# adaLN shift and scale of tiles 0, 1 and 5 as pairs from TensorE, products and tables on GpSimd, loads in order of need

## The chip, the cores and the metric

The kernel runs on one core of a Trainium2 chip. The metric is the device time of one execution in microseconds, here the median of the runs shown. The engines that matter are TensorE (PE in the profile, its weight loads PEld), VectorE (DVE), ScalarE (ACT), GpSimd (POOL) and SyncE (SP), which issues all DMAs of this kernel.

## The reference

Two layers of a decoder trunk over 256 tokens of width 1024, all in f32. What matters here is how a layer begins: the vector c gives, through `silu` and `w_mod`, a shift and a scale for each of the 1024 features, and the normed x is scaled, shifted and sent through one combined input projection.

```python
c_act = jax.nn.silu(c)
for l in range(DEPTH):
    mod = c_act @ w_mod[l] + b_mod[l]
    sh1, sc1, g1, sh2, sc2, g2 = jnp.split(mod, 6, axis=-1)
    h = modulate(rms_norm(x, mix_norm_g[l]), sh1, sc1)   # h*(1+sc1) + sh1
    y = token_mixer(h, cos_a, sin_a, cos_b, sin_b, w_in[l], ...)
    x = x + g1[:, None, :] * y
    h = modulate(rms_norm(x, ffn_norm_g[l]), sh2, sc2)
    x = x + g2[:, None, :] * channel_mixer(h, w_up[l], ffn_dw_w[l], ffn_dw_b[l], w_down[l])
```

The mixer's branches (MLA, MoBA, a convolution of 31 taps behind a GLU) use rope tables, that is the cosine and sine of positions times frequencies.

## The kernel before

The features lie on partitions: 1024 features are eight tiles of 128 (`k` = 0 to 7), and x is held as 128 x 8 x 256. Products are made in three passes for f32 accuracy: each operand is split into a rounded part and a rest (`hh` and `hl` for h, `whi` and `wlo` for a weight), and TensorE computes hi times hi, lo times hi and hi times lo (L315, L316 and L318 in `flush`).

A weight comes from memory into a buffer `raw` (one load on SP's queue), ACT makes `whi` (L231), DVE subtracts for `wlo` (L232). The function `take` does this a fixed number of weights ahead (`AHEAD0 = 2` in the first stage); `raw`, `whi` and `wlo` have four buffers each.

Layer 0 begins with a stage of its own, to about 60 us. c becomes `cact` (silu) and a row of it on every partition, `crow`. The squares of x are summed, and GpSimd's power makes rstd (`rs`). Of the modulation, the scale of tiles 0 to 3 comes from TensorE: `mod_first` (L441) loads four pieces of 512 KB, multiplies them with `cact` as stationary operand, 32 columns for each of four column groups of the array (L453), copies, transposes (L460) and adds the bias (L463). The shift of these tiles, and both for tiles 4 to 7, come from DVE: `prepare_tile` loads a row tile of 512 KB (`wmr`) for each and takes its dot with `crow` in one SCALAR_TENSOR_TENSOR with an accumulator (L816, a "dot" below), then adds the bias (L818), multiplies x by rstd into `xn` (L827, the tile `mq` in rows) and makes the gain (L823, `gs`).

The loop over the eight tiles then has ACT make h (L891, `e`) and `hh` (L892), DVE `hl` (L893), and TensorE two projections: `latents(k)` (a weight of 672 columns, 12 matmuls into `psb` banks) and `conv_in(k)` (1024 columns, 24 matmuls into four `psa` banks). Behind the loop follow the evacuations of the latents, the GLU (`glu`: tanh on ACT, `upad` on DVE), and QKV's first projection, which needs two `psa` banks.

Each engine works its instructions in the order of the program. The order is made when the kernel is built, by a scheduler that follows the source's order, dependencies and its own estimates; `issue_after(i)` puts the instructions of a block behind `i` on the same engine. So an instruction that waits holds up all that stand behind it on its engine. That goes for SP's queue too: a load that waits for its buffer holds up the loads behind it. Before the first tile PE works through `warm` matmuls (L338, "fillers" below) that nothing reads; tile 0's `latents` stand behind the last of them.

Of the kernel before, what the change touches and what calls it, by code (L numbers as in the profile page):

```python
# [158 lines left out]
def trunk_kernel(ctx, tc, xT, crow, ccol, pos, invf, modb_d, cols_d, grow_d, wmh, wmr, wm, win1, wqkv,  # L159
# [61 lines left out]
    def split(raw, lead):  # L221
# [6 lines left out]
        with ExitStack() as es:  # L228
            for i in (pins.pop(0) if pins else hold[0] or []):
                es.enter_context(tc.issue_after(i))  # L230
            ac.activation(hi, raw, AF.Copy)  # L231
            ve.tensor_tensor(lo, raw, hi.bitcast(F32), op=ALU.subtract)  # L232
# [207 lines left out]
    def mod_first(l, r, after):  # L440

        raws = []
        for i, tag in enumerate(("qkT", "lh0", "qkT", "lh1")):
# [4 lines left out]
        yield
        acc = psa()
        with tc.issue_after(after[0].ins):  # L450
            for k in range(KD):
                for c in range(4):
                    last = te.matmul(acc[32 * c:32 * c + 32, 0:P], cact[:, k:k + 1].to_broadcast([P, 32]),  # L453
                                     raws[k // 2][:, k % 2, c * P:(c + 1) * P], start=(k == 0), stop=(k == KD - 1),
                                     tile_position=(0, 32 * c))
# [3 lines left out]
        pt = psa()  # L459
        tr = te.transpose(pt[:, 0:P], g[:, 0:P], ident)  # L460
        with tc.issue_after(tr.ins):
            wlast[:] = [warm(wbank[0], WARM0[2])]
        yield ve.tensor_tensor(mod[l][:, r * 8:r * 8 + 4], pt[:, 0:P].rearrange("p (c m) -> p c m", c=4)[:, :, 0],  # L463
# [1090 lines left out]
```

## Time and profile before

| | us |
|---|---|
| median of three runs | 902.13 (901.48 to 904.43) |
| the profiled execution | 905.91 |
| its span | 903.7 |

| first stage, profiled execution | us from the span's start |
|---|---|
| four loads of `wmh`, issued | 3.06 to 5.4 |
| first matmul of the modulation | 10.25 |
| fillers | 15.16 to 18.35 |
| first matmul of tile 0 | 18.68 |
| first matmul of tile 7 | 54.84 |
| first matmul of QKV | 60.05 |

A row of a timeline has start, duration, engine, line, operation, the tile that is written and those that are read, shape and count, and in brackets how long the engine had been idle and what ended that. A row with a count over 1 merges instructions that follow each other. Pipelined instructions overlap by some hundredths of a microsecond, so the step from one to the next is a little less than a duration.

### The profile page before, as it was taken

To read this page: it belongs to the slowest core of one execution; us is meant where nothing else is said; L and a number is where in the kernel's file an instruction comes from. 1 tells how busy PE (TensorE), PEld (TensorE's weight loads), DVE (VectorE), ACT (ScalarE), POOL (GpSimd) and SP (SyncE) were. 2 spreads that over 40 slices of the span, in tenths; PEclk is the share of its full clock that TensorE was granted. 3 is DMA by queue.
4 is the path that set the end of the run, shared out by engine and by line. 5 is a ranking of instruction groups with operands and counts; after the bars stand their busy time and mean duration, and the time that the engine had idled before them with its cause. 6 is when DMAs were issued, how large, how long until landed. Compare 5 with 4: busy or idle time off the path is not lost.

```text
span 903.7 us, 18611 instructions
## 1 busy us (share of the span) xinstructions
PE 884.4 (98%) x7247; PEld 839.6 (93%) x7247; DVE 808.1 (89%) x1592; ACT 559.3 (62%) x998; POOL 47.0 (5%) x36
## 2 busy tenths in 40 slices
PE   8999999999999999999999999999999999999998
PEld 6888888999997999999989988989999999999998
DVE  6989999999987999999774999999987899998774
ACT  4677588644755655556543676787465777556551
POOL 1010700000000000000000033000000000000000
PEclk8999999999999999999999999999999999999999
DMA  8956535699888889996652666156866576886631
GB/s 320 375 202 205 187 118 175 207 330 316 309 285 286 288 287 314 316 306 228 204 161 77 200 196 200 49 167 230 274 200 209 160 233 188 301 280 205 191 95 47
DMA packets 57976, 201.59 MB, mean 223 GB/s; under 512 B 6944, under 2 KB 8480, under 8 KB 57888
## 3 DMA queue, kind: packets, MB, share of 16 engines
q1 hardware_dynamic: 57888, 200.41, 66.5%
q8 instruction: 57, 0.93, 0.4%
q14 instruction: 31, 0.25, 0.1%
HBM read 199.33 MB, written 1.05 MB: 222 GB/s over the span
## 4 chain that ended last, share of the span: by engine, by line
PE 78%; DVE 11%; DMA 5%; ACT 3%; issue 2%; SPq 0%; POOL 0%; DVEq 0%; ACTq 0%; POOLq 0%
PE psb L315 16%; PE psb L316 15%; PE psb L318 15%; PE psa L315 8%; PE psa L316 8%; PE psa L318 8%; DVE wlo L232 3%; DVE cacc L1141 2%; ACT whi L231 1%; DVE raw L816 1%; PE psa L423 1%; PE psa L734 1%; PE psa L746 1%; DMA raw<-in_win 1%; DMA raw<-in_wmh 1%
## 5 line engine op out<-in xcount | busy, mean ns | idle before, releaser
L231 ACT ACTIVATE whi<-raw 128x1024 fp32r<-128x1024 f32 (+2 forms) x286 | 296.0, 1042 | 194.4 <-PE psb L316 98.5
L232 DVE TENSOR_TENSOR wlo<-raw,whi 128x1024 fp32r<-128x1024 f32 (+2 forms) x286 | 340.3, 1195 | 50.7 <-ACT whi L231 42.4
L315 PE MATMUL psb<-hh,whi 128*128 128x256 f32 x1056 | 256.0, 282 | 0.5 <-ACT p L713 0.3
L316 PE MATMUL psb<-hl,whi 128*128 128x256 f32 x1056 | 253.7, 280 | 0.0
L315 PEld LDWEIGHTS psb<-hh,whi 128*128 128x128 f32 x1056 | 198.9, 189 | 5.0 <-issue 2.6
L316 PEld LDWEIGHTS psb<-hl,whi 128*128 128x128 f32 x1056 | 199.0, 189 | 0.5 <-DVE wlo L232 0.4
L318 PE MATMUL psb<-hh,wlo 128*128 128x256 f32 x1056 | 145.0, 279 | 0.0
L318 PEld LDWEIGHTS psb<-hh,wlo 128*128 128x128 f32 x1056 | 131.7, 188 | 0.8 <-issue 0.8
L1141 DVE SCALAR_TENSOR_TENSOR cacc<-upad,cw,cacc 128x256 f32<-128x256 f32 x240 | 105.8, 478 | 0.4
L315 PE MATMUL psa<-mhl,whi 128*128 128x256 f32 x400 | 94.2, 278 | 0.0
L316 PE MATMUL psa<-mhl,whi 128*128 128x256 f32 x400 | 94.0, 278 | 0.0
L1423 DVE SCALAR_TENSOR_TENSOR e<-psb,fw,e 128x255 f32<-128x255 f32 (+1 forms) x168 | 80.0, 478 | 6.6 <-ACT e L1421 6.0
L536 POOL TENSOR_TENSOR rs<-rs,mhalf 128x8 f32<-128x8 f32 (+3 forms) x26 | 45.5, 1761 | 678.0 <-DVE rs L535 677.9
L315 PEld LDWEIGHTS psa<-mhl,whi 128*128 128x128 f32 x400 | 75.1, 188 | 0.0
L316 PEld LDWEIGHTS psa<-mhl,whi 128*128 128x128 f32 x400 | 75.0, 188 | 0.0
L406 DVE SCALAR_TENSOR_TENSOR raw<-raw,crow 128x1024 f32<-128x1024 f32 x56 | 68.3, 1220 | 0.9 <-DMA raw<-in_wmr 0.9
L1421 ACT ACTIVATE e<-psb,fb,fw 128x256 f32<-128x256 f32 x84 | 46.5, 554 | 23.6 <-DVE e L1423 20.1
L318 PE MATMUL psa<-mhl,wlo 128*128 128x256 f32 x400 | 54.0, 278 | 0.0
L318 PEld LDWEIGHTS psa<-mhl,wlo 128*128 128x128 f32 x400 | 49.5, 188 | 0.0
L1431 ACT ACTIVATE mhl<-e 128x256 fp32r<-128x256 f32 x44 | 18.4, 417 | 39.7 <-DVE e L1429 38.0
L315 PE MATMUL psb<-whi,hh 128*128 128x416 f32 (+1 forms) x96 | 30.9, 350 | 2.9 <-ACT hh L892 2.9
L315 PE MATMUL psa<-hh,whi 128*128 128x256 f32 x128 | 30.0, 281 | 0.0
(295 smaller groups left out, 1522.2 us busy)
## 6 DMA issues: line engine op xcount, KB each, us to landing
raw<-in_wup SPq DMA_DIRECT2D x88, 512.0 KB, 4.9
raw<-in_wmr SPq DMA_DIRECT2D x68, 512.0 KB, 5.4
raw<-in_wdn SPq DMA_DIRECT2D x44, 512.0 KB, 4.6
raw<-in_wgab SPq DMA_DIRECT2D x32, 512.0 KB, 5.0
raw<-in_wqkv SPq DMA_DIRECT2D x24, 512.0 KB, 4.7
raw<-in_wm SPq DMA_DIRECT2D x24, 512.0 KB, 4.7
raw<-in_win SPq DMA_DIRECT2D x16, 512.0 KB, 4.5
raw<-in_wgc SPq DMA_DIRECT2D x16, 512.0 KB, 4.4
```

Source lines behind the costliest of these rows:

```text
L231: ac.activation(hi, raw, AF.Copy)
L232: ve.tensor_tensor(lo, raw, hi.bitcast(F32), op=ALU.subtract)
L315: te.matmul(o, p1[0], p1[1], start=start, stop=False)
L316: te.matmul(o, p2[0], p2[1], start=False, stop=False)
L318: last = te.matmul(o, p3[0], p3[1], start=False, stop=stop)
L406: ve.scalar_tensor_tensor(raw, raw, scale, row, op0=ALU.mult, op1=ALU.mult, accum_out=acc)
L423: te.matmul(acc[32 * c:32 * c + 32, 0:S], cact[:, k:k + 1].to_broadcast([P, 32]), raw[:, c * S:(c + 1) * S], start=(k == 0), stop=(k == KD ...
L536: gp.tensor_tensor(r, r, mhalf[:, :n], op=ALU.pow)
L1141: ve.scalar_tensor_tensor(aj, upad[:, j, t:t + S], cw[:, j * 31 + t:j * 31 + t + 1], aj, op0=ALU.mult, op1=ALU.add)
L1421: ac.activation(t, src, AF.Identity, scale=fw[:, 2, c:c + 1], bias=fb[:, c:c + 1])
L1423: ve.scalar_tensor_tensor(t[:, d:S], src[:, 0:S - d], fw[:, 2 - d, c:c + 1], t[:, d:S], op0=ALU.mult, op1=ALU.add)
L1431: ac.activation(mh, th, AF.Copy)
```

## The change

`TK = (0, 1, 5)` names three tiles whose shift and scale both come from TensorE. For each, `mod_pair` loads two pieces of 512 KB (the columns of shift and scale for this tile, the rows in two halves), multiplies both halves in one pass over the array's four column groups, and a matmul with `pick` adds the halves and turns them to two columns. One bank holds all three results. The other five tiles get both values as dots. In bytes that is six pieces of `wmh` and ten row tiles where there were four and twelve.

```diff
-        raws = []
-        for i, tag in enumerate(("qkT", "lh0", "qkT", "lh1")):
-            t = wk.tile([P, D], F32, tag=tag, ...)
-            sy.dma_start(t, wmh[:, 2 * i:2 * i + 2, :])
...
+        kt, raws = TK[i], []
+        for h in range(2):
+            tag, bufs = (("lh0", "lh1")[h], 1) if i == 1 else ("qkT", 2)
...
+            sy.dma_start(t, wmh[i, :, 4 * h:4 * h + 4, :])
...
+        acc = mbank[0][:, i * 160:i * 160 + 160]
         with tc.issue_after(after[0].ins):
+            for h in range(2):
+                for k in range(4):
+                    for c in range(2):
+                        o = 32 * (2 * h + c)
+                        last = te.matmul(acc[o:o + 32, 0:P], cact[:, 4 * h + k:4 * h + k + 1].to_broadcast([P, 32]),
+                                         raws[h][:, k, c * P:(c + 1) * P], start=(k == 0), stop=(k == 3),
+                                         tile_position=(0, o))
         g = e1()
         ac.activation(g[:, 0:P], acc[:, 0:P], AF.Copy)
         yield last
-        tr = te.transpose(pt[:, 0:P], g[:, 0:P], ident)
+        tr = te.matmul(acc[:, P:P + 2], g[:, 0:P], pick, start=True, stop=True)
+        if i == 0:
+            with tc.issue_after(tr.ins):
+                wlast[:] = [warm(wbank[0], WARM0[2])]
```

The products of x and rstd for tiles 1 to 7, the bases of the rope tables and layer 0's tables go from DVE to GpSimd, and in the source the tables move from behind the loop to behind tile 2. For tile 0, ACT makes `hh` straight from `xn`, and DVE computes h once more for `hl`.

```diff
-                with tc.issue_after(mods0[-1].ins) if k else ExitStack():
-                    ve.tensor_tensor(xn[k // 4][:, k % 4, :], x[:, k, :], bcs, op=ALU.mult)
+            ve.tensor_tensor(xn[0][:, 0, :], x[:, 0, :], bcs, op=ALU.mult)
+            for k in range(1, KD):
+                gp.tensor_tensor(xn[k // 4][:, k % 4, :], x[:, k, :], bcs, op=ALU.mult)
...
-            ve.tensor_copy(dst[:, 0, :, 0:w], cs)
+            gp.tensor_copy(dst[:, 0, :, 0:w], cs)
...
-                    ve.tensor_tensor(t[:, i, :, qk, :], base[:, i, :, :],
+                    (ve if l else gp).tensor_tensor(t[:, i, :, qk, :], base[:, i, :, :],
```

The weights of the stage are loaded two tiles ahead, with three more tags of buffers lent to them (`kv`, `vb`, `lh2`: four buffers, free in this stage), each tile's modulation before its two weights; `grow`, the factors of the tables, comes after tile 4's. Tile 7 does `conv_in` ahead of `latents`. `pins` puts chosen weight splits behind given instructions.

```diff
+    raw_tags = [("raw", 4), ("kv", 2), ("raw", 4), ("vb", 1), ("raw", 4), ("lh2", 1)]
...
+            def load_tile(k):
+                if k in TK:
+                    pes[k] = mod_pair(TK.index(k), lat_last)
+                    step(pes[k])
+                else:
+                    for r in range(2):
+                        raws0[r, k] = wload_row(0, r, k, (SPARE[len(raws0) % 4], 1))
+                preload()
+                preload()
...
+            if k + 2 < KD:
+                load_tile(k + 2)
+            if k == KD - 1:
+                conv_in(k)
+            elif k + 1 in pes and k:
+                lat_last[:] = [convl]
+                step(pes[k + 1])
             with tc.issue_after(wlast[0].ins) if k == 0 else ExitStack():
-                latents(k)
+                lat_last[:] = [latents(k)]
+            if k + 1 in pes and not k:
+                step(pes[k + 1])
...
             if k + 1 < KD:
-                prepare_tile(k + 1)
-            conv_in(k)
+                with tc.issue_after(los[-2].ins if k == 1 else last.ins):
+                    prepare_tile(k + 1)
+                make_tile(k + 1)
+                if k in (0, KD - 2):
+                    pins[:] = [[i.ins for i in tiles[k + 1]]]
+                convl = conv_in(k)
```

The first place to look at is DVE's queue before tile 4's modulation, from tile 3's `hl` to tile 4's. `raw` with `crow` is a dot, `mod0` the add of the bias, `mq` the product with rstd, `gs` the gain; `wlo` 128x1024 is a lo split for `conv_in`, 128x672 for `latents`. Before:

```order
L893 TENSOR_TENSOR hl_7_136<-e1_77_479,hh_6_135 128x256
L816 SCALAR_TENSOR_TENSOR raw_81_501,m0_83_505<-raw_81_501,crow_3_122 128x1024
L816 SCALAR_TENSOR_TENSOR raw_82_503,m0_83_505<-raw_82_503,crow_3_122 128x1024
L515 COPY cs2b_105<-trig_103 128x2x32
L516 TENSOR_SCALAR cs2b_105<-trig_103 128x2x32
L818 TENSOR_TENSOR mod0_100<-m0_83_505,modb_94 128x2
L827 TENSOR_TENSOR mq_31_257<-x_93,e1_32_258 128x256
L823 SCALAR_TENSOR_TENSOR gs_84_509<-mod0_100,col_12_146 128x1
L232 TENSOR_TENSOR wlo_87_515<-raw_85_512,whi_86_514 128x1024
L232 TENSOR_TENSOR wlo_91_549<-raw_89_546,whi_90_548 128x672
L893 TENSOR_TENSOR hl_7_136<-e1_88_542,hh_6_135 128x256
```

The same place now, from tile 2's `hl` to tile 3's; tile 4's round reads alike, and so does tile 2's behind the last split for tile 1.

```order
L948 TENSOR_TENSOR hl_7_142<-e1_68_409,hh_6_141 128x256
L874 SCALAR_TENSOR_TENSOR raw_60_379,m0_80_486<-raw_60_379,crow_3_128 128x1024
L874 SCALAR_TENSOR_TENSOR raw_61_381,m0_80_486<-raw_61_381,crow_3_128 128x1024
L233 TENSOR_TENSOR wlo_76_450<-raw_62_383,whi_75_449 128x672
L877 TENSOR_TENSOR mod0_100<-m0_80_486,modb_94 128x2
L233 TENSOR_TENSOR wlo_84_497<-raw_63_385,whi_83_496 128x1024
L858 SCALAR_TENSOR_TENSOR gs_81_490<-mod0_100,col_10_148 128x1
L948 TENSOR_TENSOR hl_7_142<-e1_82_492,hh_6_141 128x256
```

The product with rstd has left the place between add and gain, and the lo split for `conv_in` has come there; nothing stands between gain and `hl` any more. In the rounds of tiles 5, 6 and 7 the gain stands ahead of that split.

The second place is SP's queue from the first loads of the modulation on. `wmh` are pieces for TensorE, `wmr` row tiles for dots, `win1` the stage's weights. Before:

```order
L446 DMA raw_9_139<-in_wmh 128x1024
L446 DMA raw_10_141<-in_wmh 128x1024
L446 DMA raw_11_143<-in_wmh 128x1024
L382 DMA modb_94<-in_modb 128x96
L388 DMA col_12_146<-in_cols 128x343
L391 DMA grow_13_148<-in_grow 128x192
L204 DMA raw_35_279<-in_wmr 128x1024
L204 DMA raw_45_296<-in_win1 128x672
L204 DMA raw_48_302<-in_win1 128x1024
L204 DMA raw_51_308<-in_win1 128x672
L204 DMA raw_54_326<-in_wmr 128x1024
```

And now:

```order
L469 DMA raw_9_145<-in_wmh 128x1024
L392 DMA modb_94<-in_modb 128x96
L398 DMA col_10_148<-in_cols 128x343
L205 DMA raw_11_150<-in_win1 128x672
L205 DMA raw_12_152<-in_win1 128x1024
L469 DMA raw_13_154<-in_wmh 128x1024
L469 DMA raw_14_156<-in_wmh 128x1024
L205 DMA raw_15_158<-in_win1 128x672
L205 DMA raw_16_160<-in_win1 128x1024
L205 DMA raw_42_290<-in_wmr 128x1024
L205 DMA raw_43_292<-in_wmr 128x1024
```

The first weight has moved ahead by 1.6 MB: two pieces of 512 KB, `grow` (96 KB) and a row tile of 512 KB no longer stand before it.

More of the change, by code (lines that the diff above doesn't have):

```diff
@@ L52 @@
 COLAT = 0
+TK = (0, 1, 5)
 WARM0 = (10, 12, 14)
@@ L277, in trunk_kernel, with preload, fetch @@
     ahead = [AHEAD0]
-    coming, ready = list(all_units())[::-1], []
+    coming, ready, loaded = list(all_units())[::-1], [], []
+    def preload():
+        loaded.append(wload_unit(coming[-1 - len(loaded)][0]))
+    def fetch(n):
+        while coming and len(ready) < n:
+            src, ks, lead = coming.pop()
+            raw = loaded.pop(0) if loaded else wload_unit(src)
+            ready.append((split(raw, lead), src.shape[1] // len(ks), ks))
     def take(n=1):
-        while coming and len(ready) < n + ahead[0]:
-            src, ks, lead = coming.pop()
-            ready.append((split(wload_unit(src), lead), src.shape[1] // len(ks), ks))
+        fetch(n + ahead[0])
         res = []
@@ L458, in mod_first @@
         yield last
[L459 to L463, printed above, removed]
-                               modb[:, l, r * 8:r * 8 + 4], op=ALU.add)
+        tr = te.matmul(acc[:, P:P + 2], g[:, 0:P], pick, start=True, stop=True)
+        if i == 0:
+            with tc.issue_after(tr.ins):
+                wlast[:] = [warm(wbank[0], WARM0[2])]
+        rk = "p (r k) -> p k r"
+        yield ve.tensor_tensor(mod[0][:, 0:16].rearrange(rk, r=2)[:, kt, :], acc[:, P:P + 2],
+                               modb[:, 0, 0:16].rearrange(rk, r=2)[:, kt, :], op=ALU.add)
     def mod_parts(*parts):
@@ L499, in make_trig @@
         for kt, c in ((kh, c1), (kk, c1), (kh, c2), (kk, c2), (kh, c3), (kk, c3), (kh, c4)):
-            ve.scalar_tensor_tensor(ang, kt, -c, ang, op0=ALU.mult, op1=ALU.add)
+            last = ve.scalar_tensor_tensor(ang, kt, -c, ang, op0=ALU.mult, op1=ALU.add)
+            if c == c2 and kt is kk:
+                yield last
         ve.tensor_scalar(ang[:, 96:192], ang[:, 96:192], math.pi / 2.0, None, op0=ALU.add)
@@ new lines, in prepare_tile @@
+            def prepare_tile(k):
+                if k in pes:
+                    step(pes[k])
+                else:
+                    accs = small(2, "m0", 4)
+                    for r in range(2):
+                        ve.scalar_tensor_tensor(raws0[r, k], raws0[r, k], 1.0, crow0[0], op0=ALU.mult, op1=ALU.mult,
+                                                accum_out=accs[:, r:r + 1])
+                    rk = "p (r k) -> p k r"
+                    mods0.append(ve.tensor_tensor(mod[0][:, 0:16].rearrange(rk, r=2)[:, k, :], accs[:, 0:2],
+                                                  modb[:, 0, 0:16].rearrange(rk, r=2)[:, k, :], op=ALU.add))
+                tile_gain(k)
```

118 lines of the change are left out of this document (65 added, 53 removed).

## The prediction

> **What bounds the kernel now.** I read the page's busy times first, then the windows of the first stage, then the timelines of PE, DVE and ACT there, because the diff touches nothing behind that stage.
>
> ```profile
> span 903.7 us, 18611 instructions
> PE 884.4 (98%) x7247; PEld 839.6 (93%) x7247; DVE 808.1 (89%) x1592; ACT 559.3 (62%) x998; POOL 47.0 (5%) x36
> 15.00:18.00 3.00, 3.00 (x16) 2.06 (x15) 2.56 (x8) 1.57 (x3) 0.00 (x0) 0.50 1.03 411
> 20.00:30.00 10.00, 8.49 (x68) 8.28 (x67) 9.55 (x16) 6.41 (x10) 0.00 (x0) 1.00 0.99 347
> 40.00:50.00 10.00, 8.93 (x69) 8.51 (x68) 9.54 (x19) 5.37 (x9) 0.00 (x0) 1.00 0.94 379
> 130.00:904.00 774.00, 762.84 (x6434) 733.94 (x6433) 689.49 (x1320) 473.77 (x840) 23.80 (x15) 1.00 0.67 221
> ```
>
> In a window row stand: length, busy time (count) of PE, PEld, DVE, ACT, POOL, then the granted clock, the DMA share, GB/s. From 130 us on PE works 762.84 of 774 us, so what the first stage saves or loses arrives at the end nearly one to one. In the stage itself DVE is busy 9.5 of 10 us, POOL stands idle, the transfers fill 0.94 to 0.99 of the DMA engines, and PE has holes.
>
> The starts of the eight tiles on PE show these holes:
>
> ```profile
> 10.25 1.27 PE L453 MATMUL psa<-raw,cact 128*32 128x128 f32 x32
> 14.91 0.46 PE L460 MATMUL psa<-ident,e 128*128 128x128 f32 x1
> 15.16 3.19 PE L338 MATMUL psa<-warm_w 128*128 128x256 bf16 x14
> 18.68 0.78 PE L315 MATMUL psb<-whi,hh 128*128 128x416 f32 x3 [0.32 <-ACT hh L892]
> 25.08 0.78 PE L315 MATMUL psb<-whi,hh 128*128 128x416 f32 x3 [1.50 <-ACT hh L892]
> 29.79 0.65 PE L315 MATMUL psb<-whi,hh 128*128 128x416 f32 x3
> 31.65 0.28 PE L315 MATMUL psa<-hh,whi 128*128 128x256 f32 x1
> 34.39 0.35 PE L315 MATMUL psb<-whi,hh 128*128 128x416 f32 x1
> 44.52 0.77 PE L315 MATMUL psb<-whi,hh 128*128 128x416 f32 x3 [0.56 <-ACT hh L892]
> 54.84 0.76 PE L315 MATMUL psb<-whi,hh 128*128 128x416 f32 x3
> 60.05 0.39 PE L315 MATMUL psa<-whi,hh 128*128 128x512 f32 x1
> 60.28 0.40 PE L316 MATMUL psa<-whi,hl 128*128 128x512 f32 x1
> 61.75 0.50 PE L315 MATMUL psa<-whi,hh 128*128 128x512 f32 x1 [1.07 <-DVE upad L959]
> ```
>
> A tile costs PE 34.39 - 29.79 = 4.60 us when nothing is missing (1.86 us latents, the rest conv), eight cost 36.8; the stage takes 60.05 - 18.68 = 41.4. QKV then stands still: two matmuls at a step of 0.23 us would let the third start at 60.51, and it starts at 61.75, 1.24 us lost. Who makes the holes is read from one round of DVE (tile 5) with its partner ACT:
>
> ```profile
> 39.90 1.22 DVE L816 SCALAR_TENSOR_TENSOR raw<-raw,crow 128x1024 f32<-128x1024 f32 x1
> 42.30 0.17 DVE L818 TENSOR_TENSOR mod<-m,modb 128x2 f32<-128x2 f32 x1
> 42.38 0.42 DVE L827 TENSOR_TENSOR mq<-x,e 128x256 f32<-128x256 f32 x1
> 42.72 0.15 DVE L823 SCALAR_TENSOR_TENSOR gs<-mod,col 128x1 f32<-128x1 f32 x1
> 42.79 1.22 DVE L232 TENSOR_TENSOR wlo<-raw,whi 128x1024 fp32r<-128x1024 f32 x1
> 44.20 0.86 DVE L232 TENSOR_TENSOR wlo<-raw,whi 128x672 fp32r<-128x672 f32 x1 [0.19 <-ACT whi L231]
> 44.98 0.42 DVE L893 TENSOR_TENSOR hl<-e,hh 128x256 fp32r<-128x256 f32 x1
> 45.31 1.22 DVE L816 SCALAR_TENSOR_TENSOR raw<-raw,crow 128x1024 f32<-128x1024 f32 x1
> 53.54 0.15 DVE L823 SCALAR_TENSOR_TENSOR gs<-mod,col 128x1 f32<-128x1 f32 x1
> 53.73 0.60 ACT L891 ACTIVATE e<-mq,mod,gs 128x256 f32<-128x256 f32 x1 [2.89 <-DVE gs L823]
> 54.37 0.42 ACT L892 ACTIVATE hh<-e 128x256 fp32r<-128x256 f32 x1
> ```
>
> The round is 45.31 - 39.90 = 5.41 us: two dots (with their accumulator reads) 2.40 to the add, add 0.08, x times rstd 0.34, gain 0.07, lo split of conv 1.41 with its wait, lo split of the latents 0.78, hl 0.33. While DVE splits, ACT makes e and hh, so that chain costs DVE almost nothing. It takes 54.84 - 53.54 = 1.30 us from a gain to PE's start, as tile 7 shows.
>
> **The start.** A pair needs two loads of 512 KB where four stood ahead of the first matmuls, and tile 0's first dot goes.
>
> ```profile
> 10.25 0.38 PEld L453 LDWEIGHTS psa<-raw,cact 128*32 128x32 f32 x16
> 10.87 0.38 PEld L453 LDWEIGHTS psa<-raw,cact 128*32 128x32 f32 x16 [0.25 <-DMA raw<-in_wmh]
> 14.56 0.28 ACT L457 ACTIVATE e<-psa 128x128 f32<-128x128 f32 x1 [4.60 <-PE psa L453]
> 15.41 0.16 DVE L463 TENSOR_TENSOR mod<-psa,modb 128x4 f32<-128x4 f32 x1 [2.03 <-PE psa L460]
> 15.65 0.15 DVE L649 SCALAR_TENSOR_TENSOR gs<-mod,col 128x4 f32<-128x4 f32 x1
> 45.03 1.06 ACT L231 ACTIVATE whi<-raw 128x1024 fp32r<-128x1024 f32 x1 [0.55 <-DMA raw<-in_win]
> ```
>
> The 32 matmul rows of the first two loads end at 10.25 + 1.27 = 11.52; the same position in the queue serves pair 0. Copy 0.28, then the pick matmul at about 11.9 (before, the transpose stood at 14.91). It takes less than the 0.25 us between 14.91 and the first filler at 15.16, since it moves two columns; so the fillers start near 11.95 and, at 3.19 us, end at 15.15. Adding, gain, xn and hh take 1.30 + 0.34 + about 0.5 us from the pick, to about 14: behind the fillers' cover, which leaves over 1 us. **PE starts tile 0 at 15.15, 3.53 us earlier.**
>
> **Tiles 0 to 2.** Pair 1's matmuls stand behind tile 0's latents: 15.15 + 1.86 = 17.0. At full clock 2 x 0.38 us of PE plus a tail of 0.27 (1.27 - 32 steps of 0.031) to 18.05; copy with hand-over 0.4, pick 0.4, add to gain 0.25 (row 15.41 to 15.65 of the same three instructions): gain 1 at 19.1, hh 1 at 20.35. Then, as the order stands: hi split on ACT 1.06 and 0.05 to hand over, lo 1.15, dots and add 2.40, lo of the latents 0.78, lo of conv 1.15, then only gain 2: 26.95, and PE starts tile 2 at **28.25** (29.79 before).
>
> **Tiles 2 to 4** carry the point on which the forecast rests. x times rstd is no longer between add and gain, and the lo split of conv stands there instead. ACT cannot start before that split ends, and hl, which waits for ACT, holds back the next dots. A round is 0.33 + 2.40 + 0.78 + 1.15 + 1.30 - 0.05 = 5.9 us, longer than the 5.41 of before, though 0.34 us of work are gone. Tile 3 starts at 34.15, tile 4 at **40.05** (tile 3 before: 34.39).
>
> **Tile 4 to the end.** Tile 4 holds half of pair 5's matmuls (0.38) and its pick (0.25): 5.23 us. Tiles 5, 6 and 7 have gain ahead of the lo split of conv again, and tile 5 no dots; DVE's round of 2.40 + 0.78 + 0.07 + 1.15 + 0.33 = 4.73 is just PE's 4.60. The stage ends near 45.3 + 3 x 4.6 = **59.1**, 0.95 us earlier.
>
> **Behind it.** Tile 7 does conv ahead of its latents, so the GLU (tanh, then upad) frees the second QKV bank under 1.86 us of matmuls: the 1.24 us go. The evacuations of the latents are late next; they now stand behind the tanh on ACT, and QKV's 12 matmuls of 0.23 us hide them with little to spare: 0 to 0.5 us, I take 0.1.
>
> **What costs nothing, and why.** Loads: 6 x 512 + 10 x 512 KB replace 4 x 512 + 12 x 512, the same 8 MB; grow moves behind tile 4's weights, and its tables are read only behind the stage. All loads run eight buffers ahead on SP; a dot's load now waits for the dots two row tiles earlier, which stand over 6 us ahead of need. Pair 5's matmuls add a wait on PE with all of tile 4 behind it. Up to pair 5 the queue brings 12.0 MB (x and three pairs 4 x 1.05, three row tiles 3 x 1.05, five weight tiles 5 x 0.87, small ones 0.3); at the 411 GB/s of the window above that is 29 us, from about 5 us on: there at about 34 us, matmuls at 38.8. If that cover fails, each late us is lost whole.
>
> **GpSimd** takes seven multiplies of 128x256 and sixteen small operations. The trace has no such multiply:
>
> ```profile
> 1.11 0.29 POOL masks.py:199 TENSOR_SCALAR_AFFINE_SELECT ident<-ident 128x128 f32<-128x128 f32 x1
> 66.88 0.85 POOL L536 TENSOR_TENSOR rs<-rs,mhalf 128x3 f32<-128x3 f32 x1 [0.29 <-DVE rs L535]
> 89.06 10.59 POOL L536 TENSOR_TENSOR rs<-rs,mhalf 128x16 f32<-128x16 f32 x4 [21.34 <-DVE rs L535]
> 89.49 1.21 DVE L232 TENSOR_TENSOR wlo<-raw,whi 128x1024 fp32r<-128x1024 f32 x1
> ```
>
> From below 256 elements cost 2 x 0.29 = 0.58 us, from above the power's price, (10.59 / 4 - 0.85) over 12 - 3 elements (the four have 16 and 8 in turn), 0.2 us an element, would make 51 us. I take 0.6, nearest in size and kind: tile 1's product is then there at 14, needed at 19.1; the small ones I put at 0.2 to 0.3, 4 us in all, done long before the powers around 66.88 us, which stand next on POOL. At 51 us the stage would stop; a power is a slow function and a multiply is not, so I exclude it. Whether POOL slows DVE is bounded by 0 below and by its whole time, 4.2 + 4 us, above; a gain is excluded, since nothing there makes DVE faster. I take 0: the split at 89.49 lies wholly inside a power and takes its usual 1.21 us.
>
> [...]
>
> [...]
>
> **Sum:** 0.95 + 1.24 - 0.1 = **2.1 us less**. The profiled 905.91 us (span 903.7) become 903.8. The profiled execution lies 3.8 us above the median of 902.13, so the median becomes **900.0**. A measurement here tells about 0.3%, 2.7 us, from no change.
>
> **Rivals.**
> 1. DVE does not bind in tiles 2 to 4, because the chain behind the gain is shorter than 1.30 us or the dots start earlier. With the gain's 1.15 us back in three rounds the stage ends 3.4 us sooner: 896.6; with PE alone (15.15 + 36.8 + 2 x 1.0) it ends at 54.0: 894.8. For it: DVE sheds seven products of 0.34 us, two dots of 1.2 and the tables. Against: the order is fixed. 0.13.
> 2. The lock. DVE and POOL exclude each other; of the 4.2 us of products about 2.7 fall under the fillers and DVE's waits for pair 1, 1.5 remain; the 4 us of tables come behind tile 2, on DVE's chain. Up to 5.5 us lost: 905.5. It ends slower by over 2.7 us when more than 4.8 of POOL's 8.2 us land on the chain. [...] Against: 89.49. 0.28, of which 0.17 slower. [...]
> 3. The clock. It was 0.50 from 15 to 18 us (window above); if it comes back only at 18, as before, tile 0 loses 1.5 us and pair 1 with it: 901.5. For it: fillers alone ended the half clock before. Against: PE now runs unbroken from about 11.5. 0.08, same.
>
> **How the numbers follow.** The forecast keeps 0.51; its own range is 897.5 to 902, since five steps of 0.2 to 0.5 us each are rounded and a chain of 2.1 us passes the 2.7 bound easily: 0.19 of it faster, 0.32 same. Faster 0.19 + 0.13 = 0.32, same 0.32 + 0.11 + 0.08 = 0.51, slower 0.17. The range reaches to 896 (most of rival 1) and 905.3 (most of rival 2).
>
> **What would show it.** First tile matmul near 15.2; tile 2 near 28, tile 4 near 40; ACT's e waiting 1 us or more for gs in tiles 2 to 4, with DVE idle before hl; no wait for upad in QKV. Wrong if DVE's splits take longer than 1.22 us, or start late, while POOL works (rival 2), if e no longer waits for gs (rival 1), or if the clock is 0.50 past 15.5 (rival 3). A wait of PE for wmh in tile 4 would break the cover of the loads.

## The result, and the profile after

| | before | after |
|---|---|---|
| median of 6 runs, us (lowest to highest) | 902.79 (900.56 to 904.43) | 912.38 (907.61 to 913.86) |
| profiled execution, us (span) | 905.91 (903.7) | 913.86 (912.1) |
| QKV's first matmul, us from the span's start | 60.05 | 64.80 |
| first power of 128x2 | 223.73 | 232.93 |
| from there to the end of the span | 680.0 | 679.2 |

The changed kernel takes 1.0104 [1.0077, 1.0132] times as long as before: some 9.6 us more, where 900.0 us and a range to 905.3 were forecast. The two marks tell where to look. Of the time that came on, 4.75 us are there when QKV starts (3.5 after the 1.24 us stall that really went), and 9.2 us at the first power of 128x2, which comes in a later stage. From there on the two executions take the same time. So there are two losses: one in the first stage, one between 65 and 233 us. (One execution of e15 below took 4973 us and is left out of its median and ratio.)

**The first stage**, from the timeline of PE (start, us, engine, line, operation, tiles, and in brackets the idle time ahead of it with what ended it):

```profile
10.47 2.80 PE L480 MATMUL psa<-raw,cact 128*32 128x128 f32 x32
13.69 0.55 PE L486 MATMUL psa<-pick,e 128*128 128x2 f32 x2
14.10 1.75 PE L348 MATMUL psa<-warm_w 128*128 128x256 bf16 x14
16.16 0.58 PE L325 MATMUL psb<-whi,hh 128*128 128x416 f32 x2 [0.31 <-ACT hh L943]
24.59 0.35 PE L325 MATMUL psb<-whi,hh 128*128 128x416 f32 x1
32.11 0.77 PE L325 MATMUL psb<-whi,hh 128*128 128x416 f32 x3 [2.56 <-ACT hh L947]
38.07 0.77 PE L325 MATMUL psb<-whi,hh 128*128 128x416 f32 x3 [1.11 <-ACT hh L947]
42.94 1.07 PE L480 MATMUL psa<-raw,cact 128*32 128x128 f32 x16
44.98 0.76 PE L325 MATMUL psb<-whi,hh 128*128 128x416 f32 x3 [0.98 <-ACT hh L947]
51.09 0.65 PE L325 MATMUL psb<-whi,hh 128*128 128x416 f32 x3
64.80 0.40 PE L325 MATMUL psa<-whi,hh 128*128 128x512 f32 x1
65.27 0.39 PE L325 MATMUL psa<-whi,hh 128*128 128x512 f32 x1
```

Tile 0 starts at 16.16, tiles 1 to 5 at 24.59, 32.11, 38.07, 44.98 and 51.09, QKV at 64.80, and its next matmul follows without a stall. Tile 0 is earlier than before (18.68), but tile 2 is already later (29.79 before). Between the two stand DVE and POOL:

```profile
14.39 6.23 POOL L865 TENSOR_TENSOR mq<-x,e 128x256 f32<-128x256 f32 x7 [2.82 <-ACT e L851]
14.47 0.66 DVE L858 SCALAR_TENSOR_TENSOR gs<-mod,col 128x1 f32<-128x1 f32 x1
17.82 1.40 DVE L233 TENSOR_TENSOR wlo<-raw,whi 128x672 fp32r<-128x672 f32 x1
19.95 1.75 DVE L233 TENSOR_TENSOR wlo<-raw,whi 128x1024 fp32r<-128x1024 f32 x1
23.07 0.15 DVE L858 SCALAR_TENSOR_TENSOR gs<-mod,col 128x1 f32<-128x1 f32 x1
29.62 1.22 DVE L233 TENSOR_TENSOR wlo<-raw,whi 128x1024 fp32r<-128x1024 f32 x1
32.09 0.43 DVE L948 TENSOR_TENSOR hl<-e,hh 128x256 fp32r<-128x256 f32 x1 [1.18 <-ACT hh L947]
37.96 3.31 POOL L555 TENSOR_TENSOR ta<-cs2a,grow 128x64 f32<-128x64 f32 x4
```

POOL makes its seven products (`mq`) from 14.39 to 20.62, and in that stretch nearly every DVE operation is long: a gain takes 0.66 us where the one at 23.07 takes 0.15, the split of 672 columns 1.40 (before: 0.86), the split of 1024 columns 1.75, and 1.22 again at 29.62 with POOL idle. (One product, at 15.06, keeps its 0.41 us.)

**The second loss** lies in QKV's normalization, a place that the diff does not touch. POOL raises sixteen numbers a partition to a power, and DVE and PE wait for it:

```profile
97.43 0.68 DVE L1174 TENSOR_TENSOR ma<-ma,rs 128x512 f32<-128x512 f32 x1
97.52 7.84 POOL L566 TENSOR_TENSOR rs<-rs,mhalf 128x16 f32<-128x16 f32 x1 [0.59 <-DVE rs L565]
102.31 0.28 DVE L1192 COPY ma<-kr 128x256 f32<-128x256 f32 x1
105.39 0.69 DVE L1174 TENSOR_TENSOR ma<-ma,rs 128x512 f32<-128x512 f32 x1 [2.79 <-POOL rs L566]
114.61 2.08 PE L707 MATMUL psa<-qkT 96*128 96x128 f32 x8 [3.03 <-ACT qkT L1204]
```

The same power before, and the first one there:

```profile
89.06 2.90 POOL L536 TENSOR_TENSOR rs<-rs,mhalf 128x16 f32<-128x16 f32 x1 [21.34 <-DVE rs L535]
93.67 3.34 POOL L536 TENSOR_TENSOR rs<-rs,mhalf 128x16 f32<-128x16 f32 x1
```

2.90 us is the shortest such a power took (here, and both in e8 below). If that is its own work in the changed kernel too, it got going at 97.52 + 7.84 - 2.90 = 102.46, when the row of DVE operations from 97.43 to 102.59 came to its end: by this estimate it stood before a closed door for 4.94 us. Where a power gets in is estimated in the same way below. DVE then waits 2.79 us for the power and PE 3.03 us. In the windows (length, busy time of PE, PEld, DVE, ACT, POOL, granted clock, DMA share, GB/s) a second price shows, a granted clock of 0.50 behind PE's wait:

```profile
110.00:115.00 5.00, 1.82 (x13) 1.62 (x14) 5.00 (x9) 2.55 (x5) 2.09 (x1) 0.83 0.58 202
115.00:120.00 5.00, 5.00 (x17) 4.22 (x17) 3.18 (x8) 0.62 (x2) 4.04 (x3) 0.50 0.35 106
```

### The profile page after: what moved, and what is told of

It is laid out like the page before. It is cut to its first block, busy times and chain, and to the rows that moved or that the text cites. A ratio compares the mean times of both kernels' runs of the same rounds, so it can differ in the third digit from the quotient of the medians.

```text
span 912.1 us, 18687 instructions
## 1 busy us (share of the span) xinstructions
PE 887.4 (97%) x7284; PEld 842.0 (92%) x7284; DVE 806.6 (88%) x1573; ACT 557.2 (61%) x999; POOL 68.0 (7%) x59
## 4 chain that ended last, share of the span: by engine, by line
PE 79%; DVE 11%; ACT 4%; DMA 3%; issue 2%; SPq 1%; POOL 0%; DVEq 0%; ACTq 0%; POOLq 0%
PE psb L325 16%; PE psb L326 16%; PE psb L328 15%; PE psa L326 8%; PE psa L328 8%; PE psa L325 8%; DVE wlo L233 3%; DVE cacc L1222 2%; PE psa L437 1%; ACT whi L232 1%; DVE raw L874 1%; PE psa L764 1%; PE psa L776 1%; DMA raw<-in_wmh 1%; PE psa L709 1%
## 5 line engine op out<-in xcount | busy, mean ns | idle before, releaser
L566 POOL TENSOR_TENSOR rs<-rs,mhalf 128x8 f32<-128x8 f32 (+3 forms) x26 | 49.5, 1913 | 648.6 <-DVE rs L565 648.6
L326 PE MATMUL psb<-whi,hl 128*128 128x416 f32 (+1 forms) x96 | 30.4, 347 | 0.4 <-DVE hl L948 0.4
```

Source lines behind the costliest of these rows:

```text
L326: te.matmul(o, p2[0], p2[1], start=False, stop=False)
L566: gp.tensor_tensor(r, r, mhalf[:, :n], op=ALU.pow)
```

## Experiments

The theory after this reading: GpSimd's work and DVE's keep each other off. The products cost the first stage about 2 us, the tables another 1, and a power that comes into a row of DVE work without a gap is shut out and costs 6 us or more by itself. The rival: none of this is the lock; the longer stage comes from the new order (lo split ahead of the gain), and the late power is only what that delay does further down.

### What the stage loses: products, tables, order

e1 takes the seven products back to DVE, e2 the tables, e3 puts the gain ahead of the lo split of `conv_in` in tiles 2 to 4. Each leaves the rest of the change as it is.

```diff
 e1
-            for k in range(1, KD):
-                gp.tensor_tensor(xn[k // 4][:, k % 4, :], x[:, k, :], bcs, op=ALU.mult)
...
+                ve.tensor_tensor(xn[k // 4][:, k % 4, :], x[:, k, :], bcs, op=ALU.mult)
 e2
-                make_bases()
-                tables0.append(make_tables(0))
...
+            make_bases()
             with tc.issue_after(mods0[-1].ins):
+                tables0.append(make_tables(0))
 e3
+                if k in (1, 2, 3):
+                    pins[:] = [[gi[k + 1].ins]]
```

(The `ve.` line of e1 stands at the head of `prepare_tile`; in e2 the operations of both functions are `ve.`; in e3 `gi` is a list of the gains' instructions, and `...` marks lines left out, here and below.)

> The seven products of x and rstd for tiles 1 to 7 go back from GpSimd to DVE, each at the head of its tile's round; all else is the changed kernel. If DVE's two-input operations and GpSimd's products hold each other up (theory), the splits of 17 to 21.5 us take 0.85 (672 columns) and 1.22 us (1024) again instead of 1.40 and 1.75, tile 1's gain comes near 20.0 instead of 23.07, the products cost 4 x 0.34 us on DVE ahead of tiles 1 to 4, and QKV's first matmul starts near 64.80 - 3.4 + 1.4 = 62.8 us. If something else slowed DVE there, the loads above all (rival), the splits stay at 1.4 to 1.75 us, tile 1's gain comes near 23.4 and QKV starts near 66.2.

> The bases of the rope tables and layer 0's tables go back to DVE, the tables behind the loop as before; the products stay on GpSimd. If the tables on GpSimd held DVE up (theory), the round from tile 3 to tile 4 on PE falls from 6.91 to about 5.96 us, the eight small base operations lie in DVE's wait of 1.17 us before hl, and QKV starts near 64.80 - 0.95 = 63.9 us. If that round was long for another reason (pair 5's matmuls, which stay), it stays at 6.9 and QKV at 64.8 (rival). The splits at 17 to 21.5 us stay slow (1.40 and 1.75 us) in both.

> The lo split of conv for tiles 2, 3 and 4 is put behind that tile's gain on DVE; GpSimd keeps products and tables. If the order costs what the prediction said (theory), ACT's e waits 1.15 us less for the gain, DVE no longer idles before hl, each of the three rounds loses 1.15 us and QKV starts near 64.80 - 3.45 = 61.4 us. If the round is bound by something else, ACT's splits or the loads (rival), the order changes under 0.3 us a round and QKV stays at 64 or later.

**e1** took 908.98 us, 1.0078 [1.0058, 1.0097] of before, and QKV starts at 62.88. In its timeline of DVE the splits have their old length again, and the gain of tile 1 comes at 20.33:

```profile
16.06 0.85 DVE L233 TENSOR_TENSOR wlo<-raw,whi 128x672 fp32r<-128x672 f32 x1
17.09 1.22 DVE L233 TENSOR_TENSOR wlo<-raw,whi 128x1024 fp32r<-128x1024 f32 x1
20.33 0.16 DVE L858 SCALAR_TENSOR_TENSOR gs<-mod,col 128x1 f32<-128x1 f32 x1
```

From tile 0's start to this gain it takes 20.33 - 15.46 = 4.87 us, and 23.07 - 16.16 = 6.91 with the products on POOL: they cost 2.0 us there, though DVE now does them itself. The power still took 7.84 us in e1, so the products on POOL are not what shuts it out.

**e2** took 907.10 us, 1.0057 [1.0034, 1.008], QKV at 62.91 (63.9 expected). The round from tile 3 to tile 4 is 42.86 - 36.92 = 5.94 us, without the wait for `hh` at its end that the profile after shows at 44.98:

```profile
36.92 0.76 PE L325 MATMUL psb<-whi,hh 128*128 128x416 f32 x3 [1.17 <-ACT hh L947]
42.86 0.76 PE L325 MATMUL psb<-whi,hh 128*128 128x416 f32 x3
```

With the tables on POOL it is 6.91: they cost 1.0. Its ten times fall into two groups of five (903.34 to 905.57, 908.64 to 911.04); the profiled one, 911.04, has the shut-out. That the faster group had none is likely, but no profile shows it.

**e3** was a miss: 912.82 us, 1.0122 [1.0101, 1.0142], QKV at 63.04 where 61.4 was expected. Its rounds of tiles 2 and 3 do become 4.95 and 5.17 us and tile 4 starts at 40.00, but then DVE, which works in order, stands before pair 5's pick:

```profile
44.68 0.16 DVE L491 TENSOR_TENSOR mod<-psa,modb 128x2 f32<-128x2 f32 x1 [4.27 <-PE psa L486]
```

The dots of tiles 6 and 7 are queued behind it, and the 4.27 us come back as a late tile 7. The order of gain and split is therefore not worth what the rounds show; the rival falls for the whole, and keeps its part in the rounds.

### The power that is shut out

If a gap in DVE's row lets the power in, a memset of 128x1, which reads no operand, should do it. e4 puts four behind the input of the 128x16 power; e8 does the same to the kernel of before, where little is shut out; e14 and e11 repeat after and before.

```diff
+        if n == 16 and prepared.get(1) is None:
+            with tc.issue_after(rst[0].ins):
+                for i in range(4):
+                    ve.memset(small(1, "m0", 4), 0.0)
         gp.tensor_tensor(r, r, mhalf[:, :n], op=ALU.pow)
```

> Behind the 128x16 rstd input of both halves of the MLA queries DVE gets four tiny memsets (128x1), so that it runs no operation with two inputs for about 0.25 us when GpSimd is called; nothing else differs from the changed kernel. If the power of 7.84 us at 97.52 was kept out by DVE's unbroken row of two-input operations (theory), it takes 2.9 to 3.4 us here, PE's wait of 3.03 us for the transposed queries near 114.6 and the half clock there go, and the time falls from 912.4 by 4 to 5 us to about 908; QKV's start stays at 64.8. If GpSimd's power is slow there by itself (rival), it keeps its 7 to 8 us and the time stays at 912 to 913.

> Control: the kernel before with the same four memsets behind the power's input. Its powers of 16 columns were not shut out (2.90 and about 3.3 us), so the pause frees nothing: the powers keep these durations and the time is that of the kernel before within 0.3% (theory). If the memsets help or move the MLA stage by themselves (rival), the time changes by more than 2.7 us.

> The changed kernel once more, for its profile. Theory: pair 0's matmuls end late only in some executions, so tile 0 starts at 14.9 to 15.0 us as in e2 to e4 (16.16 in the first profile), QKV near 63.5 us, and the power of 128x16 near 96 us is shut out again (over 7 us, PE idle about 3 us near 113 us) if the time is 911 or more, and not if it is near 907. Rival: the first stage is late by itself, QKV at 64.8 us again, or the time is 911 or more with a power of under 4 us there.

> The kernel before, profiled once more, since its first profile (905.91 us) lay 4 us above its median. From the first 128x8 power of MoBA's b = 0 (105.61 us in the first profile) the program took 798.1 us to the end. Theory: executions differ in that rest, not in the first stage; here QKV's first matmul starts at 60.0 to 60.3 us again, and the rest takes 794 to 796 us if the time is near the median of 902. Rival: the first stage itself differs by 2 us or more between executions.

**e4**: 906.58 us, 1.0047 [1.003, 1.0064], where about 908 was expected. The power takes 3.38 us, and QKV starts at 63.54, about as late as in e14. So a late stage alone does not shut the power out. **e8**: 902.61 us, 0.9998 [0.9979, 1.0018], the powers 2.90 us each: the memsets cost nothing and gain nothing where nothing is shut out. **e14** shows the same picture as after (910.93 us; power 7.84, PE's wait 3.04, QKV 63.77, tile 0 at 15.16), so it belongs to the kernel; only some 1 us of QKV's delay in the profile after does not (64.80 against 63.77). **e11** gave 899.71 with 674.3 us behind the second mark, where the first profile of before had 680.0: a single execution is worth no more than some 3 us either way in that part.

The four memsets of e4 take 0.07 us in all (96.02 to 96.09; 0.25 expected). They also moved DVE's order: the lo split now follows the first product (L1174 in after) at once, as it does before. Two more runs were to take that apart: e16 puts the memsets behind that product, with nothing ahead of the power, and e17 has only another order and no memset. But in e16, too, the split follows the first product.

```diff
 e16
...
+            if l == 0 and b == 0:
+                with tc.issue_after(mi.ins):
+                    for i in range(4):
+                        mi = ve.memset(small(1, "m0", 4), 0.0)
+            with tc.issue_after(mi.ins):
...
 e17
+            with tc.issue_after(los[-3].ins) if l == 0 and b == 0 else ExitStack():
+                ve.tensor_tensor(q3[:, :, 64:96], q3[:, :, 64:96], ...)
...
```

> The changed kernel with nothing ahead of the power: a memset of 128x1 stands on DVE behind the first product with rstd (L1174, b = 0), that is behind the two-input operation that runs when GpSimd is called, and three more behind the lo split that follows. Theory (GpSimd gets in at the first moment without a two-input operation of DVE): the second power of 128x16 takes 2.90 + 0.5 = 3.4 us instead of 7.84, PE's wait of 3.03 us for qkT goes, and the time is 907 to 908 instead of 912.4. Rival: GpSimd must be called into a break to get in, so it stays out for the whole row of DVE's operations, 7 to 8 us, and the time stays at 911 to 913.

> The changed kernel without any memset, with another order behind the power's call: the product on q, the product on k, the lo split, the second product on q, a copy, where the changed kernel has both products on q, the split, the rope products. Theory (GpSimd gets in where DVE's row of two-input operations breaks, if only for the hand-over to a split that waits for ACT's half, or at the copy with one input): the power gets in behind the second product (about 1.1 us late, 4.0 us in all) or at the copy (about 2.7 us late, 5.6 us in all), and the time falls by 2 to 5 us. Rival: it stays out as long as before (7.8 us), whatever the order, and the time stays at 911 to 913.

**e16**: 904.90 us, 1.0037 [1.0018, 1.0056]; **e17**, on the same chip beside the same runs of before: 911.61 us, 1.011 [1.0083, 1.0137]. First e16's rows, with its windows, then e17's:

```profile
96.16 3.35 POOL L566 TENSOR_TENSOR rs<-rs,mhalf 128x16 f32<-128x16 f32 x1 [0.49 <-DVE rs L565]
96.06 0.68 DVE L1174 TENSOR_TENSOR ma<-ma,rs 128x512 f32<-128x512 f32 x1
96.69 0.06 DVE L1179 MEMSET m<- 128x1 f32 x1
96.69 1.23 DVE L233 TENSOR_TENSOR wlo<-raw,whi 128x1024 fp32r<-128x1024 f32 x1
110.00:115.00 5.00, 4.99 (x36) 4.39 (x36) 4.92 (x12) 2.04 (x5) 5.00 (x4) 1.00 0.39 111
115.00:120.00 5.00, 5.00 (x38) 4.07 (x37) 5.00 (x12) 4.64 (x20) 0.95 (x1) 1.00 0.35 110
```

```profile
96.15 6.29 POOL L566 TENSOR_TENSOR rs<-rs,mhalf 128x16 f32<-128x16 f32 x1 [0.32 <-DVE rs L565]
98.73 0.29 DVE L1193 COPY ma<-kr 128x256 f32<-128x256 f32 x1
102.48 0.69 DVE L1174 TENSOR_TENSOR ma<-ma,rs 128x512 f32<-128x512 f32 x1 [1.23 <-POOL rs L566]
```

In e16 the power gets in at 96.16 + 3.35 - 2.90 = 96.61, where the first DVE product ends. PE has no hole, and the granted clock stays 1.00. The changed kernel took 9.6 us more than the runs of before beside it, e16 3.7 (904.90 against 901.24; 907 to 908 had been expected): this puts the shut-out and what follows from it at about 6 us. The marks agree: from QKV's first matmul to the first power of 128x2 it is 167.0 to 168.1 us in the five profiles whose power takes 7.83 or 7.84 us (after, e14, e1, e2, e3), 165.1 in e17, and 161.0 to 162.5 in e4, e5 and e16.

That the memset is what lets the power in is not shown. In e4 the memsets, at 96.02, stand ahead of the power, called at 96.15, and it gets in at 96.15 + 3.38 - 2.90 = 96.63, behind the first product, as in e16. What the two have in common with before is ACT: the split behind that product starts 0.03 us after ACT has ended its `whi`. e1 has the same order of product and split and no memset, but there ACT was 0.14 us ahead. Two rows of before, one of e16 (its split is shown above), three of e1:

```profile
93.10 1.06 ACT L231 ACTIVATE whi<-raw 128x1024 fp32r<-128x1024 f32 x1 [1.68 <-PE psb L316]
94.19 1.22 DVE L232 TENSOR_TENSOR wlo<-raw,whi 128x1024 fp32r<-128x1024 f32 x1
95.59 1.06 ACT L232 ACTIVATE whi<-raw 128x1024 fp32r<-128x1024 f32 x1 [1.45 <-PE psb L326]
94.86 1.06 ACT L232 ACTIVATE whi<-raw 128x1024 fp32r<-128x1024 f32 x1 [1.42 <-PE psb L326]
95.56 7.84 POOL L566 TENSOR_TENSOR rs<-rs,mhalf 128x16 f32<-128x16 f32 x1 [0.32 <-DVE rs L565]
96.07 1.21 DVE L233 TENSOR_TENSOR wlo<-raw,whi 128x1024 fp32r<-128x1024 f32 x1
```

In all profiles kept, a boundary ahead of a split opened for the second power of 128x16 when `whi` had ended 0.03 to 0.13 us before the split began (0.03 in before, e4 and e16, 0.13 in e12), and stayed shut when it had ended 0.14 us or more before (0.14 in e1, 0.20 in e2, 0.45 in after). e17 fits: the power gets in only at 96.15 + 6.29 - 2.90 = 99.54, at the seventh boundary between two DVE operations, ahead of a split at 99.60 whose `whi` ends at 99.56. At its first split, at 97.26, `whi` had been done since 96.80, and the COPY at 98.73 opened nothing on either side. So e17 was a miss in size: 4.0 or 5.6 us for the power and 2 to 5 us less time had been expected, and the time is that of after. (ACT's leads are differences of rows rounded to 0.01 us.) No run changed ACT's lead alone, and powers of 128x8 elsewhere get in behind a split without such a wait: that of before at 105.61 takes 2.61 us where 1.63 is the shortest, and so gets in at 106.59, where a split ends whose `whi` had been done 0.38 us before it began. So this is what the open boundaries have in common, not a proven cause.

### Without GpSimd in the stage

e5 puts products and tables back on DVE and has the memsets (its repeats are e12 and e13); e6 adds e3's order; e9 is e6 with pairs for tiles 0, 1 and 2 instead of 0, 1 and 5; e15 adds to e9 one DVE order (add, gain, lo split of conv, `hl`) for tiles 2 to 7.

```diff
 e9
-TK = (0, 1, 5)
+TK = (0, 1, 2)
 e15
...
+                if k:
+                    pins[:] = [[gi[k + 1].ins]]
+                    fetch(3)
+                    make_tile(k + 1, los[-1].ins)
...
```

> Products, bases and tables all go back to DVE, and the four memsets stand behind the power's input; pairs, loads and the order of the splits stay as changed. If GpSimd's work in the first stage costs what the first four runs say (theory), tile 2's round is as with the products on DVE (29.7), rounds 2 to 4 take 5.96 + 0.34 = 6.3 us without tables on GpSimd, QKV starts at 60.4 to 61.0 us, about 2.9 us ahead of the run with the pause alone (63.54), and the time falls from 906.6 to about 903.7. If GpSimd's share is smaller (rival), QKV starts at 62.5 or later and the time stays near 906.

> The kernel of the run before, with the lo split of conv for tiles 2 to 4 behind the gain as well. Theory: the rounds of tiles 2 to 4 fall to 5.3 us each (tile 4 near 39.5), but tile 5's gain waits on DVE for pair 5's pick, which PE makes 4.4 us after it starts tile 4, and DVE's four dots for tiles 6 and 7 stand behind it; so most of the 3 us are lost again by tile 7, QKV starts only 0.5 us earlier than in the run before and the time is the same within 1 us. Rival: the order is what holds the stage, QKV starts 2.5 to 3 us earlier and the time falls to about 901.

> The kernel of e6 (all of GpSimd's new work back on DVE, pause, gain ahead of the split) with tiles 0, 1 and 2 as pairs instead of 0, 1 and 5, so that DVE takes no dots before tile 3 and PE no pair in tile 4. Theory (the first stage is bound by DVE's dots that stand early, and pair 5 costs PE 2.1 us where PE has none to give): tile 2 starts near 25.5 us instead of 29.3, the rounds of DVE behind it take 5.3 us, QKV starts at 57 to 58 us and the time is 3 to 5 us under that of e6 (905.5), 901 to 902 or less. Rival: the loads are what binds now (DMA share 0.97 up to about 50 us), tile 2's pair comes late, QKV starts at 60 us or later and the time stays within 1.5 us of e6.

> The kernel of e5 once more, for its profile. Theory (the rest of the loss lies behind 224 us, in stretches that the order made by the scheduler moves): the power near 224 us starts at 223.5 to 224.8 us, and from there to the end the program takes 678 to 681 us, against 674.3 and 680.0 us in the two profiles of the kernel before. Rival: it starts at 226 us or later, a power of the MLA stage takes over 7 us or the start is late.

> The same kernel a third time, with the same expectations: theory 223.5 to 224.8 us at that power and 678 to 681 us behind it; rival 226 us or later there.

> The kernel of e9 (pairs for tiles 0, 1 and 2, GpSimd's work on DVE, pause), with one order of DVE's queue in all tiles from 2 to 7: add, gain, lo split of conv, hl, so that ACT makes e and hh under the split; in e9 tiles 5 to 7 had hl ahead of that split and PE waited 1.04 and 1.11 us for hh there. Theory: these two waits go, the rounds fall from 5.8 and 6.0 to about 5.2 us, QKV starts near 59 us instead of 60.73, and the time falls by 1.5 to 2 us against e9 (903.4), to about 901.5, level with the kernel before or a little under it. Rival: loads or ACT bind in these tiles, QKV starts after 60.3 us and the time stays at 903 to 904.

| | QKV starts | median, us | ratio [95%] |
|---|---|---|---|
| e5 | 61.56 | 905.82 | 1.0039 [1.002, 1.0059] |
| e12, e13 (one run each) | 62.84, 62.76 | 905.91, 906.13 | |
| e6 | 64.07 | 905.51 | 1.0028 [1.001, 1.0045] |
| e9 | 60.73 | 903.40 | 1.0009 [0.9994, 1.0023] |
| e15 | 60.09 | 902.16 | 1.0000 [0.9984, 1.0016] |

e5 was expected at 903.7, with QKV at 60.4 to 61.0, and missed: its time is the rival's (near 906), and so is QKV in the repeats (62.5 or later). Against e4, taking all of GpSimd's new work back gives 0.7 to 2.0 us at QKV and 0.8 us in the time, less than the 2.0 and 1.0 us that the work costs where it runs. Without GpSimd's work tile 1's weight seems to bind next. ACT waits for its landing, as e12 shows (e5 has 1.85 there, 1.17 less, and QKV 1.28 us earlier):

```profile
18.40 0.77 ACT L232 ACTIVATE whi<-raw 128x672 fp32r<-128x672 f32 x1 [3.02 <-DMA raw<-in_win]
```

e6's stage came later, not 0.5 earlier, at the same time: e3's loss again. e9's tile 2 was expected at 25.5 and starts at 28.87 (28.53 in e15, where tile 0 starts 1.06 us earlier), so the third pair gives less than it seemed, and part of that is spent behind it, on `hh` of tiles 6 and 7:

```profile
28.87 0.35 PE L325 MATMUL psb<-whi,hh 128*128 128x416 f32 x1
49.23 0.77 PE L325 MATMUL psb<-whi,hh 128*128 128x416 f32 x3 [1.04 <-ACT hh L951]
55.21 0.74 PE L325 MATMUL psa<-hh,whi 128*128 128x256 f32 x4 [1.11 <-ACT hh L951]
```

e15 is the best version of the change that was found. It has QKV at 60.09 (59 expected) without the stall, and ties with before. No version is faster than the kernel before. In e12 and e13 the first power of 128x2 starts at 224.49 and 225.34, and the rest takes 679.3 and 678.7 us (223.5 to 224.8 and 678 to 681 expected), which lies between the two executions of before, 674.3 and 680.0: a loss behind that mark cannot be told.

### One part alone, on the kernel of before

e7 moves only the seven products to GpSimd; e10 only does `conv_in` ahead of `latents` in tile 7.

```diff
 e7
-                with tc.issue_after(mods0[-1].ins) if k else ExitStack():
+                if not k:
                     ve.tensor_tensor(xn[k // 4][:, k % 4, :], x[:, k, :], bcs, op=ALU.mult)
+                    for j in range(1, KD):
+                        gp.tensor_tensor(xn[j // 4][:, j % 4, :], x[:, j, :], bcs, op=ALU.mult)
 e10
-                latents(k)
+                (conv_in if k == KD - 1 else latents)(k)
...
-            conv_in(k)
+            (latents if k == KD - 1 else conv_in)(k)
```

> The kernel before, with one part of the change alone: the seven products of tiles 1 to 7 on GpSimd, issued behind tile 0's. If the two engines exclude each other (theory), DVE's two-input operations beside the products take 0.3 to 0.5 us longer each than in the kernel before until the products end, the products take about 0.9 us instead of 0.6 there, tile 1 starts later than 25.08 us or at the same time, and DVE wins 0.34 us a round behind it, 2 us in all: QKV starts at 58.5 to 60 us. If they don't (rival), no DVE operation is longer than before and QKV starts 7 x 0.34 = 2.4 us earlier, at 57.7.

> The kernel before with one part of the change alone: tile 7 does conv ahead of its latents. Theory: the wait of 1.07 us for upad in QKV goes, tile 7 starts PE's work at the same time, and the time falls by about 1.2 us (0.13%), less than can be told well. Rival: the latents' evacuation stands later on ACT and takes the gain back, the transposes of the latents wait for ma and the time is that of the kernel before.

**e7**: 903.77 us, 1.0023 [1.0004, 1.0043]. QKV starts at 61.42, 1.37 us later than before, where 58.5 to 60 had been expected, though DVE has 7 x 0.34 = 2.4 us less to do. The size was missed; that the two engines' work is longer side by side shows in POOL's group, a dot beside it and a dot behind it:

```profile
15.52 8.61 POOL L829 TENSOR_TENSOR mq<-x,e 128x256 f32<-128x256 f32 x7 [4.26 <-ACT e L805]
16.52 1.75 DVE L816 SCALAR_TENSOR_TENSOR raw<-raw,crow 128x1024 f32<-128x1024 f32 x1
27.91 1.22 DVE L816 SCALAR_TENSOR_TENSOR raw<-raw,crow 128x1024 f32<-128x1024 f32 x1
```

A product takes 1.23 us in the mean (0.73 to 1.76), a dot 1.75 us, 0.53 more than the one behind the products.

**e10** settled nothing: 909.19 us, 1.008 [1.0047, 1.0112]. The scheduler drew QKV's first matmul into tile 7 (56.15, behind 1.80 us of wait for `whi`), and PE waits 1.23 us for `qll` at 69.15, so this is not the edit alone. In the changed kernel itself the stall is gone.

## Why the prediction was wrong

- **The start** held. PE begins tile 0 at 15.16 in e14 and 14.89 in e16; 15.15 was forecast. The pick comes later (12.91 in e14 instead of 11.9), and the fillers take less (1.69 instead of 3.19 us), which cancel. In the profile after, tile 0 starts at 16.16, 1.01 us late, and that is the clock: 0.71 from 10 to 12 us and 0.50 from 12 to 14, where e14 has 1.00, and pair 0's matmuls take 2.80 us instead of e14's 2.16. It is not rival 3, whose half clock was to last to 18 us: here it ended before the fillers did (1.00 from 14.5 us on, the fillers to 15.85).
- **Tiles 0 to 2** were 2.85 us short beside the start's 1.01: gain 1 stands 6.91 us behind tile 0's start, forecast 3.95. Of the 2.96, 2.0 are the cost of the products on POOL (e1), and 0.9 were mis-sized in e1 too: there tile 0's latents took 2.32 us to pair 1's matmuls, not 1.86, and those 1.54 us, not 1.03 (0.76 and a tail of 0.27). From gain 1 to tile 2 it is 9.04 us (9.15).
- **Tiles 2 to 4**: the round of 5.9 us was right (5.96 from tile 2 to 3), with `hl` idle 1.18 us as forecast. The next one takes 6.91, since the tables fall into it (e2: 1.0 us).
- **Tile 4** takes 6.11 us instead of 5.23. Each half of pair 5's matmuls occupies PE for 1.07 us, not 0.38. **Tiles 5 to 7** take 13.71 us (13.8). In sum 1.01 + 2.85 + 0.06 + 1.01 + 0.88 - 0.09 = 5.7 us, which is 64.80 - 59.1.
- **The GLU's stall** went as forecast: 0.47 us between QKV's first two `whi,hh` matmuls and no wait for `upad`.
- **The step that failed is "I take 0"** for what GpSimd does to DVE, with its proof: "the split at 89.49 lies wholly inside a power and takes its usual 1.21 us". The row is right and the inference wrong: that power was under way already, with its 2.90 us, and left the split alone. Not every power of 128x16 is of that length, and this was to be read on POOL, where the second one took 3.34 us (7.84 in after); the group's mean of 10.59 / 4 hid it. And the split stands beside a power, not a multiply: beside the products most of DVE's operations were some 0.5 us longer (the gain 0.51, the splits 0.54 and 0.53). In place of the 0 the runs showed 2.0 us for the products (e1) and 1.0 for the tables (e2), each in its own round.
- **"The diff touches nothing behind that stage"** was the second failure. True of the text; but the timing and order of DVE's work around the powers changed, and one of them is now shut out. That is worth about 6 us (e16), half of the 12.4 us between forecast and result. If the wait for ACT decides, it could hardly have been forecast: between e1 (shut) and e12 (open) lies 0.01 us.
- **Rival 2** had a chance of 0.28 and 905.5 us: e16, with the shut-out away, took 904.90. That the numbers meet is partly luck: its 5.5 us were to come from the lock alone, and GpSimd's work cost 3.0 us in the rounds. That DVE and POOL exclude each other is not shown as such. The long splits beside the products (1.75 for 1.22 us) and the power of 7.84 us agree with it; the split at 89.49, with its usual 1.21 us inside a power, does not.

In e16 QKV starts at 63.52, 3.47 us later than before, and the stall of 1.24 is gone, which makes 2.2 us. Its measured loss is 0.18% to 0.56%, 1.6 to 5.0 us, so the stage explains it within the measurement. Two things stay open: whether 1 to 2 us more are lost further behind, where the scheduler's order of DVE also differs, and why e5, whose QKV starts 1.96 us before e16's (61.56, 63.52), is no faster than e16 (905.82, 904.90). Its lead is gone at the first power of 128x2 already (224.08, 224.51).

## What to carry to other kernels

Before work goes to GpSimd to relieve DVE, count it on both: look for the same operation's length with and without the other engine's work beside it, on each side, and one by one, not in a mean over a group. Look also at where a small operation on GpSimd that others wait for falls in DVE's row: the same power of 128x16 took 3.34 us in before and 7.84 in after, and the edit was in another stage. In these traces the open places and the shut ones lay close together: ACT's `whi` had ended 0.13 us before the split in e12 (open) and 0.14 in e1 (shut). When the loss is larger than the stage that was edited, place marks along the whole timeline before forming a theory.

## What the hardware showed unexpectedly

- A power of 128x16 on GpSimd took 2.90 us in before (at 89.06), and 7.84 in after (at 97.52), where it came into a row of some ten DVE operations with no gap (97.43 to 102.59): with 2.90 us as its own work, it got none of the boundaries between them.
- Where the power got in behind the first product, the split that followed began 0.03 us after ACT's `whi` had ended (before, e16). The step from the product to the next operation was 0.62 us in before (93.57 to 94.19) and 0.63 in e16 (96.06 to 96.69), both open, and 0.60 in e1 (95.47 to 96.07), shut. A memset of 128x1 (0.06 us) stood there in e16 and not in before, so it is not needed; whether it would open a boundary by itself, no run shows.
- A multiply of 128x256 on GpSimd took 0.73 us at least, and 1.23 in the mean beside DVE (e7). The sixteen small operations, put at 4 us in all, take from 33.79 to 44.60 us in the profile after: the four 128x64 products of one table 3.31 us.
- A wait of PE of 3.03 us was followed by about 5 us at a granted clock of 0.50 (in e14, behind 3.04 us, 0.70 from 115 to 120 us; in e16, without the wait, 1.00). So the profile after has two losses against e16: 26.41 us of PE work from 100 to 130 us instead of 29.96, and the slow clock on top. That the wait brought the clock down is not shown by itself.
